# Pool mixer of a two-layer decoder: x kept by features, modulation columns on TensorE, unread products as fillers

## The chip, the core and the metric

The kernel runs on one core of one Trainium2 chip. Its engines are TensorE (PE, with its weight loads shown as PEld), VectorE (DVE), ScalarE (ACT), GpSimd (POOL) and SyncE (SP), which issues most of the loads. The metric is the device time of one execution in microseconds, lower is better. A profile is one further execution, with the hardware profiler on.

## The reference

A decoder of two layers over 512 tokens of 1024 features in fp32. Layer 0 mixes tokens by averages over windows (the pool mixer), layer 1 by a gated unit over chunks (SGU); a squared-ReLU MLP of width 4096 follows each. Shift, scale and gate of every layer come from the condition `c`. What the change touches is layer 0's mixer and the start of its MLP:

```python
mod = silu(c) @ ada_w[i] + ada_b[i]                 # 6 x 1024 numbers
sh1, sc1, g1, sh2, sc2, g2 = split(mod, 6)
h = rmsnorm(x, norm_mix_g[i]) * (1 + sc1) + sh1
# pool mixer: group g of 256 features, window 2, 4, 8, 16 tokens
pooled[g] = mean of the last win tokens of h[g] - h[g]
y = concat(pooled[g] @ pool_w[g]) * pool_scale
x = x + g1 * y
h = rmsnorm(x, norm_mlp_g[i]) * (1 + sc2) + sh2
x = x + g2 * (square(relu(h @ w1[i])) @ w2[i])
```

## The kernel before, in words

Large products are made in fp32 precision out of a rounded high part and a remainder, in three passes (`mm3`: low weights by high data, high by high, high by low). `x` lies in SBUF by tokens, four tiles `X(t)` of 128 tokens by 1024 features in two halves `x_98` and `x_99` (in the code `x_[0]`, `x_[1]`); `xf` is x by features, eight columns `k` of 128 features by 512 tokens.

The stage in question is the mixer, from the start to the first matmul of the MLP of layer 0. It is written in one block whose order is set by hand in two tables: `LOADS` (line 53) names the loads in the order in which SP issues them, `WORK` (line 63) names the pieces of work. A piece is a letter code and digits: `m20` is a modulation column (group 2, number 0), `win2` the window products of group 2, `pd2` their eviction, `pr2` the product with the pool weights, `ad21` the addition into x (group 2, half 1), `sm23` the squares of group 2 in token tile 3, `tn2` the transposes into xf and `td2` their copies, `n00` a column of the MLP's modulation. A suffix V puts a piece on DVE. Each engine runs its own instructions in the order in which the pieces stand. Modulation weights come as 128x1024 tiles into 13 slots (3 `ada`, 5 `wh`, 5 `wl`), and a load is issued when its slot is free.

A *column* (line 694) is one DVE instruction over such a tile: 128 outputs on the partitions, times the row `silu(c)` spread over the partitions (`cb`), summed along the row. Three of the four gate groups are made on PE instead (`gm`, line 720): eight matmuls of 128x256 with `cab` (silu(c) repeated over 128 columns) as weights give the gate by features in a row, the same on all partitions. The fourth (`gt`, `gc`, `bc`) takes two DVE columns and spreads them by a diagonal and a matmul with ones. `we` (743) multiplies gate and pool scale into the pool weights.

The sums of squares of x (`sq`) go to one power on POOL (`rms`), which scales the four bands (`bandr`); a window product is x by tokens times a band. The pooled features, by features, are the weights of `product` (768), which gives tokens by features; `add` (778) adds into x by tokens. Each of x's 256-feature groups is then squared by tokens (`sm`), transposed into xf and copied. The total (`tot`) goes to a second power on POOL, to a diagonal (`diag`) and a spread over all partitions (`rb`). `norm_hi` (854) makes the MLP's operand `ht` and its high part `hb`.

Where PE would wait, `busy` (620) issues matmuls that nobody reads (`BUSY`, line 74: 10 of 128x128, the others 128x256).

Both halves of x are written to DRAM (`spill`, 530) right before the sweep; the last part of layer 0's MLP reads them. The *sweep* runs the first seven of the MLP's 32 column blocks with k outermost: eight steps of 21 matmuls of 512 columns. Each step also needs a raw weight tile, whose high part is copied on ACT (`wh`) and whose low part is made on DVE (`wl`), and two further columns. What follows the sweep is ordered by a planner (`Plan`) from a table of costs, and by the order of the code in layer 1.

In the profile every instruction that goes through the engines' wrapper outside of the planned part has line 107, in the planned part line 135 (102 and 130 in the changed kernel).

Of the kernel before, what the change touches and what calls it, by code (L numbers as in the profile page):

```python
# [7 lines left out]
F32 = mybir.dt.float32  # L8
# [26 lines left out]
V_C, V_ADAB, V_MIX, V_MLP, V_N = 0, 8, 104, 120, 136  # L35
# [10 lines left out]
def c_g(n, k):  # L46
# [18 lines left out]
    pr2 win3 m10 gc1 m11 bc1 ad21 m13 gm0 ad20 sm23 fin1 m33 we1 pd1 win0 m01 sm22 m02 m00 m03 pr1 ad10  # L65
    fin0 pd0 m32 gm3 m30 we0 pr0 m31 fin3 sm10 pd3 ad11 we3 sm21 sm11 hi0 pr3 sm20 ad00 sm13 sm12 sm01
    ad01 sm02 sm03 n00 tn2 sm00 tn0 ad30 s3 ad31 n01 sm30 sm31 sm33 sm32 td2 tot td0 tn3 nf0 n21 n11 tn1
    diag td3 td1 sp0 sp1 lo0
"""


GM = [0, 2, 3]
GT = [1]
BUSY = {"rowc": 10, "gm2": 7, "win2": 3, "gm3": 2, "rb": 2, "sweep": 4}
EARLY = 2

# [277 lines left out]
def decoder_kernel(ctx: ExitStack, tc: tile.TileContext, xtok, vecs, rows, fgrow, ada0, adag, ada1, pool_w, w1s, w1, w1f, w1b, w2, w2e, w_v, w_u, w_o, wsT, lnp, bs, out):  # L354
# [28 lines left out]
    def bank(name, pool=None):  # L383
        pool = pool or ps
        return pool.tile([P, S], F32, name=name, tag="mm" if pool is ps else "xz")
# [184 lines left out]
    with (  # L570
# [5 lines left out]
        for r in range(3):  # L576
            (Y, A)[r > 0].dma_start(row[32 * r : 32 * r + 1], rows[r : r + 1])
# [39 lines left out]
        cab = st.tile([P, KD, P], F32, name="cab")  # L617
        psb = st.tile([P, D], F32, name="psb")

        def busy(name, o, what=None):  # L620

            what = cab.rearrange("p k c -> p (k c)") if what is None else what
            n = min(256, what.shape[-1])
            for _ in range(BUSY.get(name, 0)):
                T.matmul(o[:, 0:n], ones, what[:, 0:n], start=True, stop=True)

        def spread_row(o, r, f):
            for n in range(2):
                pc = bank("pc")
                if (r, n) == (0, 0):  # L630
                    busy("rowc", pc, ones)
                T.matmul(pc, ones[32 * r : 32 * r + 1, :], row[32 * r : 32 * r + 1, S * n : S * n + S], start=True, stop=True)
                A.activation(o[:, S * n : S * n + S], pc, f)

# [3 lines left out]
        def rms():  # L638
            v0 = sm.tile([P, NT], F32, name="rv4", tag="rv4")
            V.tensor_scalar(v0, ss, RMS_EPS, None, ALU.add)  # L640
            rt.append(power(v0, NT))

        def bands():

            for t in range(NT):
                A.activation(bandr[:, t], band[:, 1 if t else 0], AF.Copy, scale=rt[0][:, t : t + 1])
# [7 lines left out]
        def places(name):  # L654

            kind = name.rstrip("0123456789")
            if kind == "n" and int(name[1]) > 1:
                return slots[0:1]
            return [slots[(nslot[0] + j) % len(slots)] for j in range({"ag": 2, "m": 1, "gt": 1, "n": 1}.get(kind, 0))]

        def load(name):
            kind, d = name.rstrip("0123456789"), [int(c) for c in name if c.isdigit()]
            for j, (pool, tag) in enumerate(places(name)):
                r = pool.tile([P, D], F32, name="ada", tag=tag) if pool is w4 else wtile(tag, F32)
                src = {"ag": lambda g: adag[GM.index(g), j], "m": lambda g, q: ada0[4 * g + q], "gt": lambda g, q: ada0[32 + 2 * GT.index(g) + q], "n": lambda k, q: ada0[16 + 2 * k + q]}[kind]
# [35 lines left out]
        pmg = [sm.tile([P, 2], F32, name="pmg", tag=f"pmg{g}", bufs=1) for g in range(4)]  # L701

        def m(g, j):

            column(f"m{g}{j}", pm4[g][:, j : j + 1])

# [8 lines left out]

        pgs, dgs = {}, {}

        def gm(g):  # L720
            po = pgs[g] = bank("pg", xz)[:, 0:256]
            busy(f"gm{g}", po)
            for j in range(2):
                r = take(f"ag{g}", j).rearrange("p (k c) -> p k c", k=4)
                for k in range(4):
                    T.matmul(po, cab[:, 4 * j + k], r[:, k], start=(j + k == 0), stop=False)
            T.matmul(po, ones[32:33, :], row[32:33, 256 * g : 256 * g + 256], start=False, stop=True)

        def gt(g, j):
            column(f"gt{g}{j}", pmg[g][:, j : j + 1])  # L730

        def gc(g):
            pm = pmg[g]
            dg = dgs[g] = st2.tile([P, 2, P], F32, name="dgg", tag="dgg")
            V.tensor_tensor(pm, pm, vec[:, V_ADAB + c_g(0, 2 * g) : V_ADAB + c_g(0, 2 * g) + 2], ALU.add)
            for j in range(2):
                A.activation(dg[:, j], ident, AF.Copy, scale=pm[:, j : j + 1])

        def bc(g):
            pgs[g] = bank("pg", xz)[:, 0:256]  # L740
            T.matmul(pgs[g], ones, dgs.pop(g), start=True, stop=True)

        def we(g):

            gp = st2.tile([P, 256], F32, name="gp", tag="gp")
            V.tensor_tensor(gp, pgs.pop(g), psb[:, 256 * g : 256 * g + 256], ALU.mult)
            c = slice(2 * g, 2 * g + 2)
            V.tensor_tensor(pw[:, c], pw[:, c], gp.unsqueeze(1).to_broadcast([P, 2, 256]), ALU.mult)
# [3 lines left out]
        def windows(g):  # L752

            for k in (2 * g, 2 * g + 1):
                po = pqs[k] = bank("pq")
                if k % 2 == 0:
                    busy(f"win{g}", po)
                for t in range(NT):
                    n = P if t == NT - 1 else W
                    T.matmul(po[:, P * t : P * t + n], X(t)[:, P * k : P * k + P], bandr[:, t, g, 0:n], start=(t == 0), stop=(t == NT - 1), skip_group_check=True)  # L760
# [7 lines left out]
        def product(g):  # L768
            for h in range(2):
                po = pos[g, h] = bank("po", xz).rearrange("p (t c) -> p t c", t=2)  # L770
                for q in range(2):
                    t = 2 * h + q
                    for j in range(2):
                        T.matmul(po[:, q], pds[2 * g + j][:, P * t : P * t + P], pw[:, 2 * g + j], start=(j == 0), stop=(j == 1))

        ssg = st.tile([P, NT, 4], F32, name="ssg")

        def add(g, h):
            c = slice(256 * g, 256 * g + 256)
            V.tensor_tensor(x_[h][:, :, c], x_[h][:, :, c], pos.pop((g, h)), ALU.add)  # L780

        def sums_of(g, t, on=A):
            squares(ssg[:, t, g : g + 1], t, slice(256 * g, 256 * g + 256), on)

        pxs = {}

        def turn(g):
# [3 lines left out]
            for h in range(2):  # L791
                for k in (2 * g, 2 * g + 1):
                    for t in (2 * h, 2 * h + 1):
                        T.transpose(pxs[k][:, P * t : P * t + P], X(t)[:, P * k : P * k + P], ident)
# [4 lines left out]


# [4 lines left out]
        def n_(k, j):  # L805
            if k not in pm2:
                pm2[k] = sm.tile([P, 2], F32, name="pm2", tag="pmv")
            column(f"n{k}{j}", pm2[k][:, j : j + 1])

# [24 lines left out]

        def sum3():
            V.tensor_reduce(s3, ssg[:, :, 0:3], mybir.AxisListType.X, ALU.add)
            V.tensor_scalar(s3, s3, RMS_EPS, None, ALU.add)

        def tot():
            V.tensor_tensor(s3, s3, ssg[:, :, 3], ALU.add)  # L840
            rt.append(power(s3, NT))

        def spread_norms():
            rbs.append(bank("rb", xz))
            busy("rb", rbs[0])
            for t in range(NT):
                r = rt[1][:, t : t + 1]
# [15 lines left out]
        def norm_32(k):  # L863
# [4 lines left out]
            rowc=lambda: spread_row(cb, 0, AF.Silu),  # L868
            rowp=lambda: spread_row(psb, 2, AF.Copy),
            cab=lambda: V.tensor_copy(cab, ca.unsqueeze(2).to_broadcast([P, KD, P])),  # L870
            sq=lambda t, on=A: squares(ss[:, t : t + 1], t, slice(0, D), on),
            sm=sums_of, rms=rms, edge=edges, bandr=bands, m=m, n=n_, nf=n_fin, fin=fin, gm=gm, gt=gt, gc=gc, bc=bc, we=we,
            win=windows, pd=pooled, pr=product, ad=add, tn=turn, td=turned, s=lambda _: sum3(), tot=tot,
# [3 lines left out]
        for op in WORK.split():  # L877
            on_v, op = op.endswith("V"), op.rstrip("V")
# [4 lines left out]

        sweep = [bank("po", xz) for _ in range(SWEEP - 4)] + [bank("po") for _ in range(4)]
        busy("sweep", sweep[0])
        for k in range(KD):
# [14 lines left out]
            norm_32(k)  # L901
            (xh, xl), (wh, wl) = apart(H(k, ALL)), wk[k][1:]
# [761 lines left out]
```

## Time and profile before

| | us |
|---|---|
| three runs: median (lowest to highest) | 824.36 (822.27 to 826.08) |
| the profiled execution | 823.1 |
| its span | 821.4 |
| PE busy in the span | 810.8 (99%) |
| DVE, ACT, POOL busy | 688.1, 484.7, 67.8 |
| first matmul of the sweep | 59.98 |
| end of the sweep in the chain of waits | 97.09 |

The span runs from the first to the last instruction of the program in the profiled execution; the execution's own time has 1.7 us around it. A timeline row merges instructions alike that follow one another ("x16"); an fp32 matmul appears as two entries, a transpose as one. The clock that the profile shows for PE is the granted one; a number in brackets at a row's end is the idle time before it and what ended it.

### The profile page before, as it was taken

The page shows a single profiled execution, that of the slowest core. Times are in us where ns is not written, and L with a number is a line of the kernel's source. Part 1 is how long each engine was busy: PE and PEld are TensorE (multiplying, and loading weights), DVE is VectorE, ACT ScalarE, POOL GpSimd, SP SyncE. Part 2 cuts the span into 40 slices and gives each one's busy share as a digit, 9 for nine tenths or more (in the row PEclk, how much of TensorE's full clock was granted, in tenths as well). Part 3 has the DMA queues.
Part 4 walks back from the last instruction along what each step waited for, and adds up shares of the span by engine and source line. Part 5 has one row for each costly group of instructions (what it writes and reads, how often), then busy time and mean ns, then how long its engine had stood idle before and what let it go on. Part 6 is the DMA issues. An engine that isn't in the chain of part 4 may idle for free.

```text
span 821.4 us, 12594 instructions
## 1 busy us (share of the span) xinstructions
PE 810.8 (99%) x4877; PEld 736.2 (90%) x4877; DVE 688.1 (84%) x924; ACT 484.7 (59%) x704; POOL 67.8 (8%) x93
## 2 busy tenths in 40 slices
PE   9999999999999999999999999999999999999996
PEld 7878889999999999888889888999999999999985
DVE  6889988899998999867798976788789988987865
ACT  4376886675656577257333227676766667677521
POOL 3000001010101010000020001010101000111001
PEclk9999999999999999999999999999999999999999
DMA  9979996889887897526755746947888889777402
GB/s 350 418 286 343 331 273 134 265 219 271 220 277 189 271 254 247 192 103 245 268 171 192 220 161 236 324 98 201 202 255 225 242 220 255 186 175 252 132 26 102
DMA packets 43792, 185.45 MB, mean 226 GB/s; under 512 B 4923, under 2 KB 5075, under 8 KB 36438
## 3 DMA queue, kind: packets, MB, share of 16 engines
q1 hardware_dynamic: 35282, 137.72, 46.1%
q0 software_dynamic: 8016, 44.58, 27.1%
q10 hardware_dynamic: 436, 2.37, 0.8%
q8 instruction: 38, 0.62, 0.3%
q14 instruction: 20, 0.16, 0.1%
HBM read 178.34 MB, written 6.30 MB: 225 GB/s over the span
## 4 chain that ended last, share of the span: by engine, by line
PE 84%; DVE 7%; DMA 3%; ACT 3%; issue 1%; POOL 0%; POOLq 0%; ACTq 0%; DVEq 0%
PE po L107 29%; PE pm L135 18%; PE pm L107 17%; PE po L135 15%; PE pg L107 2%; DMA ada<-in_ada 2%; DVE wl L107 2%; DVE ada L107 2%; DVE v L107 1%; PE pq L107 1%; PE pc L107 1%; DMA raw<-in_w_o 1%; ACT wh L107 1%; PE px L107 1%; ACT hb L107 0%
## 5 line engine op out<-in xcount | busy, mean ns | idle before, releaser
L107 PE MATMUL po<-hb,wh 128*128 128x256 f32 (+1 forms) x816 | 177.4, 314 | 0.0
L107 PEld LDWEIGHTS po<-hb,wh 128*128 128x128 f32 x816 | 134.9, 191 | 8.6 <-DVE hb L107 0.7
L107 PE MATMUL po<-hb,wl 128*128 128x256 f32 (+1 forms) x408 | 128.8, 316 | 0.5 <-DVE wl L107 0.5
L107 DVE TENSOR_TENSOR wl<-raw,wh 128x1024 fp32r<-128x1024 f32 (+2 forms) x85 | 99.0, 1170 | 30.6 <-ACT wh L107 30.3
L107 ACT ACTIVATE wh<-raw 128x1024 fp32r<-128x1024 f32 (+2 forms) x85 | 85.4, 1015 | 53.9 <-PE pm L107 23.4
L107 PEld LDWEIGHTS po<-hb,wl 128*128 128x128 f32 x408 | 77.9, 191 | 5.7 <-PE po L107 0.9
L135 ACT ACTIVATE wh<-raw 128x1024 fp32r<-128x1024 f32 x48 | 50.8, 1058 | 49.3 <-PE pm L135 18.7
L135 PE MATMUL po<-hb,wh 128*128 128x256 f32 (+1 forms) x400 | 78.1, 296 | 0.0
L135 DVE TENSOR_TENSOR wl<-raw,wh 128x1024 fp32r<-128x1024 f32 x48 | 58.3, 1220 | 10.3 <-ACT wh L135 10.0
L135 PEld LDWEIGHTS po<-hb,wh 128*128 128x128 f32 x400 | 63.7, 191 | 2.0
L107 PE MATMUL pm<-wh,oh 128*128 128x512 f32 x188 | 63.8, 357 | 0.0
L135 PE MATMUL pm<-wh,oh 128*128 128x512 f32 x188 | 63.8, 357 | 0.0
L107 PE MATMUL pm<-wh,ol 128*128 128x512 f32 x168 | 63.7, 379 | 0.0
L135 PE MATMUL pm<-wh,ol 128*128 128x512 f32 x168 | 63.7, 379 | 0.0
L135 PE MATMUL pm<-wl,oh 128*128 128x512 f32 x168 | 63.7, 379 | 0.0
L107 PE MATMUL pm<-wl,oh 128*128 128x512 f32 x168 | 63.7, 379 | 0.0
L107 DVE SCALAR_TENSOR_TENSOR ada<-ada,cb 128x1024 f32<-128x1024 f32 x48 | 58.2, 1218 | 4.7 <-DMA ada<-in_ada 4.6
L135 PE MATMUL po<-hb,wl 128*128 128x256 f32 (+1 forms) x201 | 59.3, 296 | 0.0
L107 PE MATMUL po<-as,wh 128*128 128x256 f32 x288 | 49.0, 275 | 0.0
L107 PEld LDWEIGHTS po<-as,wh 128*128 128x128 f32 x288 | 43.7, 192 | 0.0
L135 PE MATMUL po<-as,wh 128*128 128x256 f32 x240 | 40.8, 275 | 0.0
L107 PEld LDWEIGHTS pm<-wh,oh 128*128 128x128 f32 x188 | 35.5, 189 | 5.1
(269 smaller groups left out, 1893.8 us busy)
## 6 DMA issues: line engine op xcount, KB each, us to landing
ada<-in_ada SPq DMA_DIRECT2D x72, 512.0 KB, 4.5
raw<-in_w1b SPq DMA_DIRECT2D x44, 512.0 KB, 5.3
b<-in_w SPq DMA_DIRECT2D x18, 1024.0 KB, 7.1
bt<-in_w POOLq DMA_DIRECT2D x18, 1024.0 KB, 8.3
raw<-in_w1b POOLq DMA_DIRECT2D x22, 512.0 KB, 5.6
raw<-in_w2e SPq DMA_DIRECT2D x16, 512.0 KB, 4.2
bt<-in_w SPq DMA_DIRECT2D x6, 1024.0 KB, 8.7
b<-in_w POOLq DMA_DIRECT2D x6, 1024.0 KB, 9.5
```

Source lines behind the costliest of these rows:

```text
L107: return f(*a, **kw)
L135: self.ops.append((name, attr, lambda: f(*a, **kw), out, ins, kw))
```

## The change

All of it is in the mixer's stage; the sweep's arithmetic and what comes after it are the same.

- x is transposed into xf at the start of the stage (`xt`, `xd`). The product has the pool weights as weights and the pooled features as data (128x512, by features, one k at a time), so gate and pool scale are one number per partition: `add` (k) is a DVE instruction xf = po * gain + xf. `we`, `gm`, `gc`, `bc`, the spread of the pool scale and two of the three row loads are gone; the gate is eight more columns `g0` to `g7`. For the spill, x is transposed back (`bt`) and copied back (`be`).
- A column whose name carries a P in `WORK` (m13, g3, m03, g4, n01, n11) is made on PE: eight matmuls of 32 output rows, with 32 columns of `cab` as weights, at four positions of the array's columns (`tile_position`), two at each, accumulated; an ACT copy (`prt`) and a one-column matmul with `sel` (`whole`) add the four partial sums. Its tile is stored transposed in DRAM.
- Fillers (`z8` and so on) are 128x128 matmuls of ones, written into the next PSUM bank that is opened, 42 in all.
- The sums of squares for the second norm are made by tokens for three groups, and for columns 4 and 5 of group 2 as a square of the full 128x512 column (`sk`) with a matmul by ones (`ss`). First norm and bands go token tile by token tile, with four powers on POOL.
- The loads have a new order: four modulation tiles stand ahead of x. The two spills are issued from ACT at steps 6 and 7 of the sweep.

How this moves instructions on PE at the end of the stage, from the last window products to the sweep. Names: `po` products, `px` transposes, `pg` gates, `pq` windows, `pt` a column on PE, `pm` its sum, `ss` sums of squares, `rb` the spread of the norms; before:

```order
L107 MATMUL po<-pw,pd 128x256 x8
L107 MATMUL pg<-cab,ones 128x256 x2
L107 MATMUL pg<-wl,cab 128x256 x4
L107 MATMUL pg<-wh,cab 128x256 x4
L107 MATMUL pg<-row,ones 128x256
L107 MATMUL po<-pw,pd 128x256 x16
L107 MATMUL px<-ident,x_98 128x128 x4
L107 MATMUL px<-ident,x_99 128x128 x4
L107 MATMUL rb<-cab,ones 128x256 x2
L107 MATMUL rb<-diag,ones 128x128 x4
L107 MATMUL po<-cab,ones 128x256 x4
L107 MATMUL po<-hb,wl 128x512
```

and in the changed kernel:

```order
L102 MATMUL po<-pd,pw 128x512 x4
L102 MATMUL pt<-wl,cab 32x128 x8
L102 MATMUL pm<-sel,prt 128x1
L102 MATMUL px<-ident,xf 128x128 x8
L102 MATMUL ss<-ones,sqk 128x128 x8
L102 MATMUL pt<-wh,cab 32x128 x8
L102 MATMUL px<-ident,xf 128x128 x8
L102 MATMUL pt<-ada,cab 32x128 x8
L102 MATMUL pm<-sel,prt 128x1
L102 MATMUL rb<-ones 128x128 x2
L102 MATMUL rb<-diag,ones 128x128 x4
L102 MATMUL po<-hb,wl 128x512
```

The 32 transposes of x (the pair of px rows stands four times before) have left this place for the start of the stage; transposes back, three columns and the full-column sums stand here now.

On DVE, over the same stretch (`pm`, `mg` sums of columns, `gp` gate times pool scale, `wl`, `wh`, `ada` tiles of columns), before:

```order
L107 TENSOR_TENSOR gp<-pg,psb 128x256
L107 TENSOR_TENSOR pw<-pw,gp 128x512
L107 TENSOR_TENSOR x_98<-x_98,po 128x2x256
L107 TENSOR_TENSOR x_99<-x_99,po 128x2x256
L107 SCALAR_TENSOR_TENSOR wl,pm_484<-wl,cb 128x1024
L107 TENSOR_TENSOR x_98<-x_98,po 128x2x256
L107 TENSOR_REDUCE s_168<-ssg 128x4
L107 TENSOR_SCALAR s_168<-s_168 128x4
L107 TENSOR_TENSOR x_99<-x_99,po 128x2x256
L107 SCALAR_TENSOR_TENSOR ada,pm_484<-ada,cb 128x1024
L107 TENSOR_TENSOR s_168<-s_168,ssg 128x4
```

and in the changed kernel:

```order
L102 SCALAR_TENSOR_TENSOR mg<-mg,vec 128x1
L102 SCALAR_TENSOR_TENSOR xf<-po,mg,xf 128x512
L102 SCALAR_TENSOR_TENSOR mg<-pm,vec 128x1
L102 SCALAR_TENSOR_TENSOR xf<-po,mg,xf 128x512
L102 COPY x_98<-px 128x2x256
L102 SCALAR_TENSOR_TENSOR sq_148,ssg<-x_99 128x256
L102 SCALAR_TENSOR_TENSOR sq_148,ssg<-x_98 128x256
L102 TENSOR_REDUCE s_166<-ssg 128x4
L102 TENSOR_SCALAR s_166<-s_166 128x4
L102 TENSOR_TENSOR s_166<-s_166,ss 128x4
L102 SCALAR_TENSOR_TENSOR wl,pm_593<-wl,cb 128x1024
```

The additions go to xf, each behind its gain; the last one waits for a column that PE made, and only one of the MLP's columns is left on DVE ahead of the norm's spread.

The diff, cut (the two tables to their first lines):

```diff
 LOADS = """
-    x m20 ag2 m22 m21 m23 gt11 pw2 gt10 m12 m10 m13 m11 m33 ag0 m01 pw1 m02 m00 m03 m32 m30 ag3 pw0 m31
-    n11 pw3 raw0 n00 n21 n01 raw1
+    m11 m10 m13 g3 x m12 m33 g2 m31 g7 m30 pw1 m32 m23 m03 pw3 m22 g6 m20 m21 m00 m02 pw2 m01 g5 pw0 g1 g0 g4
+    n01 n00 raw0 n11 raw1
...
-    cab edge sq0 rowc sq2 sq3 sq1V rms m20 m22 rowp m21 m23 gt11 fin2 bandr gm2 win2 we2 gt10 pd2 win1 m12
+    z8 rowc z9 z1 m13P qm13 m11 sq2 g3P m10 sq0V edge z9 z7 xt2 sq1V rms0 rms2 xt1 m12 qg3 gf3 sq3V qm10 rms1
...
-BUSY = {"rowc": 10, "gm2": 7, "win2": 3, "gm3": 2, "rb": 2, "sweep": 4}
+SPIN = 5
 EARLY = 2
+SPILL = (6, 7)
...
         o = pool.tile([P, S], F32, name=name, tag="mm" if pool is ps else "xz")
+        while owed:
+            owed.pop()
+            T.matmul(o[:, 0:P], ones, ones, start=True, stop=True)
...
+        def rms(t):
+            V.tensor_scalar(v0[:, t : t + 1], ss[:, t : t + 1], RMS_EPS, None, ALU.add)
+            G.tensor_tensor(r0[:, t : t + 1], v0[:, t : t + 1], mhalf[:, 0:1], ALU.pow)
...
         def column(name, out):
             r = take(name)
-            V.scalar_tensor_tensor(r, r, 1.0, cb, ALU.mult, ALU.mult, accum_out=out)
+            if name + "P" not in WORK:
+                V.scalar_tensor_tensor(r, r, 1.0, cb, ALU.mult, ALU.mult, accum_out=out)
+                return
+            r = r.rearrange("p (k c) -> p k c", k=KD)
+            pt = bank("pt")[:, 0:P]
+            for k in range(KD):
+                q = 32 * (k % 4)
+                T.matmul(pt[q : q + 32], cab[:, k], r[:, k], start=(k < 4), stop=(k >= 4), tile_position=(0, q), skip_group_check=True)
+            parts_of[name] = st2.tile([P, P], F32, name="prt", tag="prt", bufs=4)
+            A.activation(parts_of[name], pt, AF.Copy)
+        def whole(name, out):
...
+            pm = bank("pm")[:, 0:1]
+            T.matmul(pm, parts_of.pop(name), sel, start=True, stop=True)
...
+        def gain(k):
+            gains[k] = mg[:, KD + k : KD + k + 1]
+            V.scalar_tensor_tensor(gains[k], pmg.pop(k), vec[:, V_ADAB + c_g(0, k) : V_ADAB + c_g(0, k) + 1], vec[:, V_PS + k : V_PS + k + 1], ALU.add, ALU.mult)
...
+        def product(k):
+            pos[k] = bank("po", xz)
+            g = k // 2
+            for j in range(2):
+                T.matmul(pos[k], pw[:, 2 * g + j, P * (k % 2) : P * (k % 2) + P], pds[2 * g + j], start=(j == 0), stop=(j == 1))
+        def add(k):
+            V.scalar_tensor_tensor(xf[:, k], pos.pop(k), gains.pop(k), xf[:, k], ALU.mult, ALU.add)
...
+        def sum_up(k):
...
+            q = sqk.pop(k)
+            for t in range(NT):
+                T.matmul(sums[0][:, tok[t]], q[:, tok[t]], ones, ...)
...
+        def back(g, h):
+            b = pbs[g, h] = bank("px").rearrange("p (t c) -> p t c", t=2)
+            for k in (2 * g, 2 * g + 1):
+                for q in range(2):
+                    T.transpose(b[:, q, P * (k % 2) : P * (k % 2) + P], xf[:, k, tok[2 * h + q]], ident)
...
+        fill(SPIN)
         sweep = [bank("po", xz) for _ in range(SWEEP - 4)] + [bank("po") for _ in range(4)]
-        busy("sweep", sweep[0])
         for k in range(KD):
...
+            if k in SPILL:
+                spill(SPILL.index(k), A)
```

More of the change, by code (lines that the diff above doesn't have):

```diff
@@ L575, in decoder_kernel @@
         row = st.tile([P, D], F32, name="row")
-        for r in range(3):
-            (Y, A)[r > 0].dma_start(row[32 * r : 32 * r + 1], rows[r : r + 1])
+        Y.dma_start(row[0:1], rows[0:1])
         W = P + 16
@@ L714, in fin, with gate, qg @@
             V.scalar_tensor_tensor(b0[:, k], sh, win * (1.0 / win), sh, ALU.mult, ALU.subtract)
[L718 to L748, printed above, removed]
+        def gate(k):
+            pmg[k] = mg[:, k : k + 1]
+            column(f"g{k}", pmg[k])
+        def qg(k):
+            pmg[k] = whole(f"g{k}", pmg[k])
+        def gain(k):
+            gains[k] = mg[:, KD + k : KD + k + 1]
+            V.scalar_tensor_tensor(gains[k], pmg.pop(k), vec[:, V_ADAB + c_g(0, k) : V_ADAB + c_g(0, k) + 1], vec[:, V_PS + k : V_PS + k + 1], ALU.add, ALU.mult)
         pqs, pds, pos = {}, {}, {}
```

154 lines of the change are left out of this document (86 added, 68 removed).

## The prediction, made before the changed kernel ran

> **What bounds the kernel now.** I read the page first, then the chain of waits over the first 110 us, then the windows and timelines of the mixer's stage. The page's first part names the engine:
>
> ```profile
> PE 810.8 (99%) x4877; PEld 736.2 (90%) x4877; DVE 688.1 (84%) x924; ACT 484.7 (59%) x704; POOL 67.8 (8%) x93
> ```
>
> TensorE (PE) is busy for 99% of the span, so time can be won only where PE does work that nothing needs, or before it has real work. That is the mixer's stage: the chain (start, duration, engine, tile; an "x28" counts entries) shows where it ends.
>
> ```profile
> 1.14 8.35 PE pc L107 x28
> 9.48 9.49 PE pg L107 x32
> ...
> 44.69 7.12 PE po L107 x32
> 51.83 0.70 DVE x L107
> ...
> 52.61 0.52 ACT sq L107 x2
> ...
> 53.66 0.98 ACT xf L107 x2
> ...
> 54.69 1.85 PE px L107 x14
> 56.54 1.76 PE rb L107 x12
> 58.30 38.79 PE po L107 x176
> 97.09 12.96 PE po L135 x61
> ```
>
> PE carries the chain almost unbroken to 51.8; then come one addition, squares, copies, transposes and the spread of the norms, and the sweep over the MLP's first seven column blocks begins. Its first matmul is here:
>
> ```profile
> 59.98 0.48 PE L107 MATMUL po<-hb,wl 128*128 128x512 f32 x1
> ```
>
> From 97.09 on the chain is PE alone, and the diff changes nothing after the sweep. So the change is worth what it moves the sweep's start at 59.98 and its end at 97.09. The windows (us; busy PE, PEld, DVE, ACT, POOL; granted clock, DMA share, GB/s) say what the stage is short of:
>
> ```profile
> 45.00:50.00 5.00, 5.00 (x25) 4.41 (x24) 3.15 (x5) 4.81 (x17) 0.00 (x0) 1.00 0.95 385
> 50.00:55.00 5.00, 4.29 (x30) 3.56 (x29) 4.27 (x12) 4.38 (x15) 1.06 (x1) 1.00 0.12 26
> 80.00:90.00 10.00, 10.00 (x48) 8.46 (x47) 10.00 (x17) 6.38 (x15) 0.00 (x0) 1.00 0.97 316
> ```
>
> The loads run to about 50, with the same bytes in both kernels, and PE, DVE and ACT are all loaded; no single engine has much room.
>
> **The change part by part.** The prices, one row for each kind of work (PE first, then DVE, ACT, POOL):
>
> ```profile
> 1.12 4.63 PE L107 MATMUL pc<-ones 128*128 128x128 f32 x20 [1.12 <-DVE edge L107]
> 5.69 3.79 PE L107 MATMUL pc<-row,ones 1*128 1x512 f32 x8
> 24.13 3.62 PE L107 MATMUL po<-pw,pd 128*128 128x256 f32 x16
> 33.48 0.69 PE L107 MATMUL pg<-row,ones 1*128 1x256 f32 x2
> 34.11 2.18 PE L107 MATMUL pq<-bandr,x 128*128 128x144 f32 x16
> 51.63 1.91 PE L107 MATMUL px<-ident,x 128*128 128x128 f32 x16
> 57.24 1.05 PE L107 MATMUL rb<-diag,ones 128*128 128x128 f32 x8
> 33.82 1.22 DVE L107 SCALAR_TENSOR_TENSOR wh<-wh,cb 128x1024 f32<-128x1024 f32 x1
> 34.97 1.22 DVE L107 SCALAR_TENSOR_TENSOR wl<-wl,cb 128x1024 f32<-128x1024 f32 x1
> 51.27 0.17 DVE L107 TENSOR_SCALAR s<-s 128x4 f32<-128x4 f32 x1
> 58.42 0.75 DVE L107 SCALAR_TENSOR_TENSOR ht<-xf,scl,rb 128x512 f32<-128x512 f32 x1 [0.88 <-PE rb L107]
> 5.58 1.06 ACT L107 ACTIVATE sq<-x 128x1024 f32<-128x1024 f32 x1 [2.44 <-DMA x<-in_xtok]
> 14.57 2.78 ACT L107 ACTIVATE bandr<-band,rr 128x576 f32<-128x576 f32 x4 [1.28 <-POOL rr L107]
> 30.65 1.45 ACT L107 ACTIVATE pd<-pq,b,scl 128x512 f32<-128x512 f32 x2 [1.57 <-DVE b L107]
> 50.53 0.42 ACT L107 ACTIVATE sq<-x 128x256 f32<-128x256 f32 x1
> 51.07 0.42 ACT L107 ACTIVATE sq<-x 128x256 f32<-128x256 f32 x1
> 53.57 2.05 ACT L107 ACTIVATE xf<-px 128x512 f32<-128x512 f32 x4
> 55.48 0.50 ACT L107 ACTIVATE mods<-pm,vec 128x1 f32<-128x1 f32 x2
> 56.12 0.70 ACT L107 ACTIVATE diag<-ident,rr 128x128 f32<-128x128 f32 x2
> 65.31 0.95 ACT L107 ACTIVATE wh<-raw 128x896 fp32r<-128x896 f32 x1 [1.92 <-DMA raw<-in_w1s]
> 53.94 1.93 POOL L107 TENSOR_TENSOR rr<-s,mhalf 128x4 f32<-128x4 f32 x1 [39.40 <-DVE s L107]
> 407.22 0.54 POOL L107 TENSOR_TENSOR rr<-rv,mhalf 128x1 f32<-128x1 f32 x1 [26.94 <-DVE rv L107]
> ```
>
> *Unknown price: a modulation column on PE.* Six columns leave DVE (six times 34.97 - 33.82 = 1.15 us) and become eight 32x128 matmuls each, which is 16 entries of 128 columns, with an ACT copy and a one-column matmul behind. A 128-column entry costs 1.91/16 = 0.12 us, so one after another the 16 take about 1.8 us. The nearest row for narrow work is the ones-by-row one: its eight entries of 512 columns fell in the time when 128 columns cost 0.21 us (4.63 for twenty, less the 0.4 in which the last one leaves the array), which would be 8 x 0.85 = 6.8 us; they took 3.79, so two ran at a time. I take two at a time, 0.9 us. Lower bound: four at a time, 0.45. Upper bound: the two entries of 33.48 took 0.69, against 2 x 3.62/16 = 0.45 for full entries of that shape, about 0.1 lost per entry; 16 x (0.11 + 0.1) = 3.3 us.
>
> The Trainium skill, "TensorE: Matmul & The Clock Gate", section "Part 3: Packing small matmuls — row/col tiling", gives 2.38 times the speed for three column tiles side by side; by that an operation here would be nearer 0.6 us (an estimate) and the sum about 1.5 us lower. The trace of before has no column tiles to set against it.
>
> *PE's opening.* PE starts at 1.14 as before. Eight fillers (16 entries x 0.21 = 3.4) and two row matmuls instead of four (3.79/2 = 1.9) end at 6.4, ten more fillers at 10.7; a column at that slow rate (1.8), one between the rates (1.2) and 16 fillers (32 x 0.11 = 3.5, once the entries are as short as in the px row) end at about 17, and ACT gets the first turned x at 17.2. x is loaded after four 512 KB tiles instead of first: its first tile was there at 5.58, and seven tiles more at 385 GB/s (1.36 us each) make the last one land at 15.1. That costs nothing behind those fillers, which leave it 2 us; without them PE would wait for it.
>
> *Transposes, bands, first windows.* From about 17.2 ACT has eight xf copies (2.05/4 = 0.51) and four bandr (2.78/4 = 0.70), 6.9 us: to 24.1. Of this the copies are new here (they stood at 53.57 and 57 before). The powers tile by tile (0.54 and more each on POOL, instead of 1.93 for four) end long before, beside the fillers. Seven windows that wait for the last band, at 2.18/8 = 0.27 less the overlap, 1.7, and four products of two 512-column entries (twice 3.62/16 an entry, less the overlap, so 0.86 each), 3.4, come next: to 29.2. A filler and a column, 0.2 + 0.9, to 30.3; two products, 1.7, to 32.0.
>
> *What goes.* 24 full matmuls for the gates with their rows, the diagonal and its spread, and four products with the pool weights on DVE go; they were PE's filling rather than its limit, because DVE still owes its columns.
>
> *DVE's stretch.* Two additions into xf at the price of ht (0.75 in the record, of which 0.66 until DVE takes the next), six columns at 1.15, seven small operations around the two `fin` at 0.17 or less, together 1.0, and hand-overs, 0.3: 1.3 + 6.9 + 1.3 = 9.5, to 41.5.
>
> *ACT's stretch.* Two pd (0.72), six squares (51.07 - 50.53 = 0.54), two copies back and one full-column square (0.51 each): 1.4 + 3.2 + 1.5 = 6.1, to 47.6. ACT takes its work in order: the copy of gate column 4 is queued behind these squares, and PE's matmul, DVE's gain and the last addition wait for it. Copy 0.35 (half of the diag row), one-column matmul 0.3 and gain 0.25 (as half of the mods row), addition 0.75: 1.65, to 49.3.
>
> *Tail.* Last square 0.6; eight sums with ones 1.05 (as the rb row); column 0.9, eight transposes 0.95, column 0.9; copy, copy, diagonal 0.35 + 0.25 + 0.35; spread 0.9; one-column matmul 0.3; copy, x copied back, hb 0.25 + 0.5 + 0.7. That is 8.0, to 57.3, and 0.2 for hand-overs: 57.5. POOL's power of 1.93 runs beside the columns and transposes. Loads do not decide: the same bytes end at about 50, and n01 and n11 are used after 51. The start moves from 59.98 to about 57.5, **-2.5 us**.
>
> *The sweep.* It took 37.1. At 80 to 90 it ran 48 entries in 10 us, so its 168 need 35.0 or somewhat more; the excess comes with the wait of 1.92 for the second weight tile, when two 1 MB spills stand ahead of it. The spills now go at steps 6 and 7, and the raw tile can land first. Bounds 0 and -1.9; I take **-0.8**. Sum: -3.3 us.
>
> *The moved spills.* Two issues on ACT at about 0.4 us stand in steps in which ACT is busy 6.38 of 10; what is queued behind is the next step's hb. The 2 MB meet a DMA share of 0.97: at 316 GB/s 6 us of transfer. Hidden by loads that are issued early it costs 0; without that cover PE would wait for part of it, half as an estimate, +3.
>
> **The rivals.** *Four columns at a time.* The column tiles have a quarter of the array each, and the ones-by-row entries already doubled up. At 0.45 us the five columns in the chain (two in the opening, one before 30.4, two in the tail) save 5 x 0.45 = 2.2 us more, less 0.3 that the first row of x hides: sweep from about 55.6, total -5.2, 818.5 us. Against it: no row shows more than two.
>
> *One after another.* At 1.8 the five add 4.5 us: start 62.0, less 0.8 in the sweep a total of +1.2: 824.9 us. For it: both entries of one matmul use the same quarter of the array one after the other; against it, the 3.79.
>
> *Slower: narrow matmuls lose their weight load.* If a weight load for another strip waits until the matmul in flight is out, as the 0.69 for two entries hints, an operation takes 3.3 us; five add 12 us, sweep from about 69.5, less 0.8 a total of +8.7: 832.4 us. Five operations pass the bound of +4.1 from about 0.9 + 7.4/5 = 2.4 us each on. Against it: 3.79 us for eight, on narrow tiles too.
>
> The Trainium skill, same page and section, says that a weight load overlaps matmuls in flight only when the row group differs; column tiles share their rows. "TensorEngine Tiling (Array Packing)", section "Key Properties", adds that a change of tiling mode drains TensorE. By these rules this rival would be the outcome; only the row of 33.48 agrees, at 0.1 us per entry, and the row of 3.79 does not.
>
> *The gain is eaten later.* The stage ends earlier but the loads behind the sweep land when they did, or the spills delay them: 0 net, 823.7 us. For it: the DMA share of 0.97 at 80 to 90; against it: the chain behind 97.09 shows PE alone and no transfer.
>
> **How the numbers follow.** The profiled execution took 823.1 us around a span of 821.4; the three runs have their median at 824.36, so I start from between, 823.7, and -3.3 gives 820.4. A measurement of this kernel can tell about 0.5%, 4.1 us, from no change. Chances: forecast 0.47 (over its spread of 2 us to either side about a third lies beyond -4.1), four at a time 0.20, one after another 0.12, weight loads 0.12, eaten 0.09. Faster: 0.20 + 0.17 = 0.37. Slower: 0.12 and 0.02 for the upper edge of the serial case, 0.14. Same: 0.49. The range leaves out the fastest edge of the four-fold case (start below 55 and a full 1.9 in the sweep, under 815) and the weight-load case above 829, which starts at 827.8 for 2.4 us: 815 to 829.
>
> **What would show it.** In the trace after: `pt` of eight 32x128 matmuls in 0.9 us (0.45, 1.8, 3.3 for the rivals); sweep's first `po<-hb,wl` at 57.5; ACT's second `wh<-raw` in the sweep without the wait of 1.92; the sweep's end near 93.8; PE unbroken afterwards. I am wrong if `pt` takes over 2 us, if ACT ends its squares after 49, or if the start moves and the finish does not.

## The result, and the profile after

The changed kernel takes 822.72 us (median of 20 runs, 820.76 to 825.90), the kernel before 824.09 (20 runs, 822.26 to 826.99): ratio 0.9989, 95% interval 0.9976 to 1.0002. The forecast of -3.3 us was not met: -1.4 us between the medians, not clear of zero. The forecast time of 820.4 lies below the measured median, which lies inside the stated range of 815 to 829.

The profiled execution of the changed kernel is one of its slower ones (825.6 us, span 823.9). No profile was taken of a faster execution of it. Its windows, with the columns of those shown of before:

```profile
50.00:55.00 5.00, 4.80 (x50) 4.18 (x50) 4.54 (x12) 3.70 (x12) 0.87 (x1) 1.00 0.05 20
90.00:95.00 5.00, 4.65 (x21) 3.50 (x21) 5.00 (x7) 4.04 (x6) 0.00 (x0) 1.00 0.92 347
95.00:100.00 5.00, 2.97 (x15) 2.32 (x14) 3.83 (x5) 3.46 (x6) 0.00 (x0) 1.00 1.01 397
```

The last of these windows in the kernel before:

```profile
95.00:100.00 5.00, 5.00 (x26) 4.37 (x25) 5.00 (x6) 5.00 (x10) 0.00 (x0) 1.00 0.99 416
```

The stage's end still has idle DMA queues (0.05), and PE now has a hole at 95 to 100, where before it was busy throughout. PE's timeline shows the stage's terms one by one:

```profile
4.83 3.78 PE L102 MATMUL pc<-row,ones 1*128 1x512 f32 x4
8.54 4.43 PE L102 MATMUL pt<-ones 128*128 128x128 f32 x20
12.90 0.65 PE L102 MATMUL pt<-ada,cab 128*32 128x128 f32 x16
18.50 1.91 PE L102 MATMUL px<-ident,x 128*128 128x128 f32 x16
24.51 4.05 PE L102 MATMUL pq<-bandr,x 128*128 128x144 f32 x28 [0.45 <-ACT bandr L102]
32.16 0.64 PE L102 MATMUL pt<-wl,cab 128*32 128x128 f32 x16
32.73 1.98 PE L102 MATMUL po<-pd,pw 128*128 128x512 f32 x4
51.57 2.09 PE L102 MATMUL ss<-ones,sqk 128*128 128x128 f32 x16
59.52 0.48 PE L102 MATMUL po<-hb,wl 128*128 128x512 f32 x1 [0.33 <-ACT hb L102]
```

A column on PE takes 0.57 us (32.16 to 32.73), and the two row matmuls take as long as the four did before (3.78 against 3.79). The sweep starts at 59.52, only 0.46 earlier. Its end is worse. The chain of waits and ACT's timeline there:

```profile
81.82 6.51 DMA ada<-in_ada
...
89.62 6.85 DMA raw<-in_w
96.54 1.06 ACT wh L130
...
99.08 11.07 PE po L130 x51
```

```profile
96.54 1.06 ACT L130 ACTIVATE wh<-raw 128x1024 fp32r<-128x1024 f32 x1 [2.03 <-DMA raw<-in_w]
97.51 1.04 ACT L130 ACTIVATE as<-xf 128x1024 fp32r<-128x1024 f32 x1
98.45 3.02 ACT L130 ACTIVATE g<-po 128x512 f32<-128x512 f32 x6
```

ACT waits 2.03 us for a raw tile of the part behind the sweep; the evictions of the sweep's results (`g<-po`) are queued behind that copy, and PE waits for the banks that they free. The first matmul behind the sweep's 168 stands at 99.08, against 96.93 before. The tile was issued at almost the same moment in both (89.62 and 89.48) and landed after 6.85 us instead of 4.67: the two spills were issued beside it, at 89.63 and 91.29. In all the profiles below, what follows the sweep takes 723.7 to 725.9 us, so a profile's span is set by where its sweep ends, to within about 2 us.

### The profile page after: what moved, and what is told of

It reads as the page before. It is cut to its first block, busy times and chain, and to the rows that moved or that the text cites. A ratio compares the mean times of both kernels' runs of the same rounds, so it can differ in the third digit from the quotient of the medians.

```text
span 823.9 us, 12793 instructions
## 1 busy us (share of the span) xinstructions
PE 808.9 (98%) x4969; PEld 729.9 (89%) x4969; DVE 689.3 (84%) x936; ACT 484.7 (59%) x703; POOL 70.4 (9%) x96
## 4 chain that ended last, share of the span: by engine, by line
PE 86%; DVE 7%; DMA 3%; ACT 2%; issue 1%; POOL 0%; POOLq 0%; DVEq 0%; ACTq 0%
PE po L102 32%; PE pm L130 18%; PE pm L102 17%; PE po L130 15%; DVE ada L102 2%; DVE wl L102 2%; DMA ada<-in_ada 1%; PE px L102 1%; PE pt L102 1%; PE pc L102 1%; DMA raw<-in_w 1%; DVE wh L102 1%; ACT wh L102 1%; PE pq L102 0%; DVE ht L102 0%
## 5 line engine op out<-in xcount | busy, mean ns | idle before, releaser
L102 PEld LDWEIGHTS po<-hb,wl 128*128 128x128 f32 x408 | 77.9, 191 | 5.6 <-ACT hb L102 1.3
L102 DVE SCALAR_TENSOR_TENSOR ada<-ada,cb 128x1024 f32<-128x1024 f32 x50 | 60.6, 1220 | 12.7 <-DMA ada<-in_ada 7.3
L130 PEld LDWEIGHTS po<-hb,wl 128*128 128x128 f32 x201 | 38.4, 191 | 3.4 <-ACT g L130 2.4
```

Source lines behind the costliest of these rows:

```text
L102: return f(*a, **kw)
L130: self.ops.append((name, attr, lambda: f(*a, **kw), out, ins, kw))
```

## The experiments

Sweep start and end are read from the entries on PE (the first entry, and the first behind the 168 of the sweep), as is the moment at which PE's entries become half as long ("rate up"); this moment is good to one entry, about 0.2 us. Pauses are the times from one PE entry's start to the next, added up where they are far above the regular 0.22, within the sweep and at its end. All in us, with the span of the profiled execution; the ratio is to the kernel before as measured beside the run. A row's medians come from 6 to 20 executions (one in e4 and e10), its other times from a single one, which is not always near the median.

| kernel | median | ratio (95%) | rate up | sweep start | pauses | sweep end | span |
|---|---|---|---|---|---|---|---|
| before | 824.09 | | 13.9 | 59.98 | 0 | 96.93 | 821.4 |
| changed | 822.72 | 0.9989 (0.9976-1.0002) | 12.6 | 59.52 | 3.1 | 99.08 | 823.9 |
| e1 | 822.84 | 0.9989 (0.9977-1.0002) | 5.5 | 57.75 | 0.7 | 94.73 | 818.7 |
| e2 | 823.64 | 1.0004 (0.9994-1.0014) | 5.7 | 60.65 | 0.7 | 97.66 | 823.6 |
| e3 | 822.28 | 0.9986 (0.9973-1.0000) | 12-13 | 57.28 | 2.3 | 96.36 | 820.7 |
| e4 | 833.67, one run | | 13.1 | 67.61 | 2.1 | 106.19 | 832.0 |
| e5 | 822.36 | 0.9982 (0.9974-0.9991) | 6.8 | 56.87 | 3.1 | 96.39 | 821.3 |
| e6 | 824.40 | 1.0008 (0.9992-1.0023) | 4.7 | 56.49 | 3.0 | 96.40 | 821.0 |
| e7 | 823.85 | 1.0002 (0.9991-1.0012) | 4.1 | 59.61 | 1.2 | 97.79 | 821.9 |
| e8 | 823.41 | 0.9995 (0.9979-1.0010) | 14 | 60.04 | 2.2 | 99.01 | 823.3 |
| e9 | 822.28 | 0.9986 (0.9975-0.9998) | 5.6 | 56.74 | 2.5 | 95.93 | 819.8 |
| e10 | 826.34, one run | | 4.7 | 61.65 | 2.8 | 100.61 | 824.6 |
| e11 | 819.34 | 0.9948 (0.9930-0.9967) | 4.7 | 56.76 | 0 | 93.31 | 817.0 |
| e12 | 822.49 | 0.9981 (0.9969-0.9993) | 6.4 | 56.68 | 1.6 | 94.56 | 818.3 |

The diffs below are shortened to the lines that matter.

**e1 and e2: is it the spills' place?** e1 is the changed kernel, e2 the kernel before.

```diff
 e1:  ... diag nf0 qn11 be20
+     sp0 sp1
-            if k in SPILL:
-                spill(SPILL.index(k), A)
 e2:  diag td3 td1 sp0 sp1 lo0   ->   diag td3 td1 lo0
+            if k in (6, 7):
+                spill(k - 6, A)
```

> The changed kernel with its two spills issued right ahead of the sweep, as before, instead of at steps 6 and 7. Theory 1 (the spills in the sweep take the DMA queues from the loads behind it): the two pauses of PE at the sweep's end in the changed kernel's profile (0.73 us before 92.06, 2.41 us before 99.08) go, the wait for the second raw tile near 65 comes back and costs PE 0.3 us at most, and the time falls by about 2.5 us to 819.5 to 821. Rival (the pauses are the loads' own scatter, which the spills have no part in): pauses like these appear again, and the time stays at 822.7 within 0.7.

> The kernel before with its two spills moved to steps 6 and 7 of the sweep, and nothing else. Theory 1: PE, unbroken there before, pauses for 2 to 3 us between step 7 and the end of the sweep, waiting for raw and ada tiles; the time rises to about 826. Rival: the sweep ends at 97 as before or 0.5 earlier (no wait of 1.92 near 65), the time stays at 824.1 or falls to 823.5.

The theory of the spills alone fell: by the medians e1 is no faster than the changed kernel, and e2 no slower than the kernel before. e1's profile, of one of its fastest executions (820.43), has the shorter pauses and the early end (94.73), but the sweep also *started* 1.8 us earlier, which the edit doesn't explain: PE's rate had risen at 5.5 instead of 12.6. The same rows in e1, to be set against those at 4.83 and 8.54 above:

```profile
4.83 2.27 PE L102 MATMUL pc<-row,ones 1*128 1x512 f32 x4
7.04 2.50 PE L102 MATMUL pt<-ones 128*128 128x128 f32 x20
```

Twenty entries take 2.50 us there and 4.43 in the changed kernel, with the windows' clock at 1.00 in both. That is a second cause, and it differs between executions whose opening is the same. In e2's profile, too, the rate rose early (5.7). There PE then waited 1.88 us for a gate tile, the granted clock read 0.50 from 29.5 to 32.8, and the sweep started at 60.65, later than before.

**e3: the opening.** Spills as in e1, row halves on two partitions, 16 fillers left out.

```diff
-        Y.dma_start(row[0:1], rows[0:1])
+        Y.dma_start(row[0:1, 0:S], rows[0:1, 0:S])
+        A.dma_start(row[64:65, S:D], rows[0:1, S:D])
-                T.matmul(pc, ones[0:1, :], row[0:1, S * n : S * n + S], start=True, stop=True)
+                T.matmul(pc, ones[64 * n : 64 * n + 1, :], row[64 * n : 64 * n + 1, S * n : S * n + S], start=True, stop=True)
-    ... sq0V edge z9 z7 xt2
+    ... sq0V edge xt2
```

> The changed kernel with three edits: spills ahead of the sweep; the two halves of the row of c on partitions 0 and 64, loaded by two queues, so that the two row matmuls can run side by side (3.78 us for the two in the changed kernel); and the 16 fillers ahead of the first transposes left out. Theory 2 (the stage is one chain of DVE work from about 20.6 to 51, and DVE stood idle 3.7 us before it, for a sum on PE behind those 16 fillers, after 5.3 us of waiting for cb, so each microsecond taken off PE's opening comes off the sweep's start): cb 1.8 us earlier, the idle 3.7 us gone but for 0.5, the sweep starts at 55 to 56.5 instead of 59.5, and with the spills the time is 816 to 818. Rival (the loads or the clock set the stage's end): the sweep starts at 58.5 to 60 all the same, because DVE then waits for tiles or PE falls to half clock, and only the spills' 2.5 us remain.

The start came 2.2 us earlier with a late rise (57.28, of which 1.2 us are a wait, 0.33 in the changed kernel: the spills' issues on ACT stand ahead of the first `hb`). So the chain through DVE is real. But the pauses in the sweep grew to 2.3 us and the time hardly moved: 822.28 instead of the expected 816 to 818. The rows on two strips:

```profile
4.83 2.08 PE L102 MATMUL pc<-row,ones 1*128 1x512 f32 x4
```

**e4: one strip.**

```diff
-                T.matmul(pt[q : q + 32], cab[:, k], r[:, k], start=(k < 4), stop=(k >= 4), tile_position=(0, q), skip_group_check=True)
+                T.matmul(pt[0:32], cab[:, k], r[:, k], start=(k == 0), stop=(k == KD - 1), tile_position=(0, 0))
```

> The changed kernel with the eight 32x128 matmuls of a PE column all at one position of the array (one strip of columns, one accumulation) instead of four positions in turn. By the prediction's terms: if the positions run side by side, the operation's 16 entries now take 16 x 0.11 = 1.75 us instead of 0.65, more (up to 3.3) if a load of weights for the same strip isn't hidden; the two operations in the tail move the sweep's start by 2 x 1.1 = 2.2 us, the other ones by less than 1 us. If the strips have no part in it: 0.65 us as now and no move.

```profile
13.11 1.93 PE L102 MATMUL pt<-ada,cab 128*32 128x128 f32 x16
```

1.93 against 0.65: four positions do run side by side. The start moved by 8.1 us, not 2.2: that fits six columns in the chain (6 x 1.3 = 7.8), where the expectation had two and the prediction five.

**e5, e7, e8: the rate.** e5 has 17 fillers ahead of the rows and the rows on two strips; e7 is the kernel before with 17 fillers; e8 the changed kernel again.

```diff
 e5: -    z8 rowc z9 z1 m13P        +    z9 z8 rowc z1 m13P      (and e3's rows)
 e7: -BUSY = {"rowc": 10, ...       +BUSY = {"rowc": 17, ...
```

> The changed kernel with its opening rearranged: 17 fillers ahead of the row matmuls instead of 8, one between them and the first column instead of 10, and the row's two halves on partitions 0 and 64. In the traces so far PE's entries halve in length at 5.3 to 5.6 us in two executions and at 12.5 to 13.9 in the others; the one-row matmuls stand between. Theory 3 (the rate rises after one unbroken stretch of full matmuls that fills a window of its own phase; with 8 fillers the rows break it in most executions, and the changed kernel gains only where it doesn't): with 7.2 us of fillers the rate rises by 8.4 in every execution; sweep starts at 56.5 to 57.5 (59.5 in the changed kernel's profile), the runs lose their upper group (824 to 826), median 821.0 to 821.6. Rival (the two groups of run times come from the loads in and behind the sweep): rise by 8.4 all the same, but the times spread as before over 820.8 to 825.9, median 822.7 within 0.6.

> The kernel before with 17 instead of 10 fillers ahead of its row matmuls and nothing else. In the one trace of it with the early rise PE then waited for gate tiles (0.61 at 11.48, 1.88 at 28.82) and the sweep started no earlier (60.65 against 59.98). Theory 3: the rate rises by 8.4, PE waits for loads instead, sweep start 60 to 61, time 823.7 within 0.7: the early rise is worth something to the changed kernel alone. Rival: the kernel before gains as much as the changed one, 2 to 3 us, sweep start 57 to 58.

> The changed kernel once more, for its scatter beside the others on the same chip. Theory 3: its profile shows either a rise at about 5.3 and a sweep start near 56.8, or a rise at about 12.7 and a start near 59.5, and the times lie in two groups, 820.5 to 822.5 and 824 to 826. Rival: the start doesn't follow the rise.

The first rows of e5's timeline:

```profile
1.12 6.85 PE L102 MATMUL pc<-ones 128*128 128x128 f32 x34 [1.12 <-DVE edge L102]
7.90 1.13 PE L102 MATMUL pc<-row,ones 1*128 1x512 f32 x4
8.96 0.49 PE L102 MATMUL pt<-ones 128*128 128x128 f32 x2
```

In all seven profiles with 17 full matmuls first (e5 to e7, e9 to e12) the rate rises at 4.1 to about 7; in the seven others twice early and five times at 12 to 14. The upper group of times is gone in e5 (821.08 to 823.17, against 821.07 to 827.66 in e8), and the start is 2.6 to 3.2 us earlier than in the two profiles of the changed kernel. e5 also has the rows on two strips, so not all of this is the rate; but e1, with an early rise and its rows on one strip, started at 57.75 with 0.8 us more of a wait for the spills' issues, and so would have started like e5 without it (56.9, an estimate). e7 gains nothing: it starts 0.4 earlier and its PE waits for gate tiles instead. So by these profiles the early rise is worth something only where PE's next tiles are there. But e5's median, 822.36, missed its 821.0 to 821.6: again 3.1 us of pauses at the end.

The Trainium skill ("TensorE: Matmul & The Clock Gate", section "Part 1: The HAM clock gate (the "warmup" mystery)") puts the array at half clock until one window of about 3.4 us has been busy, and lets these windows run free of the kernel's start. The runs agree where full matmuls stand alone: 17 fillers span two such windows (6.8 us) and the rise comes by 7; with 8 or 10 (3.4 and 4.3 us) it came early in two profiles of seven. But the kernel before kept PE busy without a gap from 1.12 on, and its rate rose only at 13.9, with the one-row matmuls at 5.69 to 9.48. That these don't count as busy is my inference; it wasn't tried alone.

**e6 and e9: where the spills collide least.** e6 is e5 without the 16 fillers, spills after the sweep's first step. e9 is e5 with half 0 spilled when it is turned back, half 1 behind the first `hb`.

```diff
 e6: -    z8 rowc z9 z1 m13P qm13 m11 sq2 g3P m10 sq0V edge z9 z7 xt2
     +    z9 z8 rowc z1 m13P qm13 m11 sq2 g3P m10 sq0V edge xt2
     +            if k == 0: spill(0, A); spill(1, A)
 e9: -    ... be21 bt20 qn00 n11P qn01 z2 diag nf0 qn11 be20
     +    ... be20 bt21 qn00 n11P qn01 z2 diag nf0 sp0 qn11 be21
     +            norm_hi(k); if k == 0: spill(1, A)
```

> As the kernel with the clock first, and besides the 16 fillers ahead of the first transposes left out and both spills issued from ACT at the end of the sweep's first step (ahead of the sweep they held up the first hb by 1.1 us, at steps 6 and 7 they may meet the next loads). Theory 3 with DVE's chain: first transposes at 14.7 when x lands, sweep starts at 55.5 to 56.5, 1 us ahead of the kernel with the clock first, time 819.5 to 821. Rival (x's landing and the bands hold the stage): sweep starts as in the kernel with the clock first, within 0.3.

> The kernel with the clock first (e5), and its spills where the DMA queues have nothing: half 0 issued as soon as it is turned back (the transposes back of the last group change places), half 1 right behind the sweep's first hb, which it doesn't hold up. Theory 4 (from the sweep's start the queues are full at a share of 0.9 to 1.0, so 2 MB of spill inside the sweep turn an earlier start into pauses at its end: 56.87 in e5 became 96.39, 57.75 with the spills ahead became 94.73): start at 56.9 to 57.3, pauses of 0 to 0.7 us, sweep's end at 94 to 95, the times in one group around 820.5, ratio 0.995 to 0.997. Rival (the pauses belong to the loads of an earlier start, wherever the spills are): pauses of 2 to 3 us in the sweep again, end at 96 to 97, times around 822.4 as in e5.

Starts of 56.5 and 56.7 became ends of 96.4 and 95.9; moving the spills only moved the pauses (to 66 to 72 and to 91). Theory 4 fell. Leaving out the 16 fillers brought 0.4 us at the start of e6's sweep, and the clock fell: PE waited three times for x (0.8 to 0.9 us each), and from about 12 to 18 its windows read 0.50:

```profile
12.00:14.00 2.00, 0.64 (x2) 0.18 (x1) 1.97 (x7) 1.05 (x2) 0.00 (x0) 0.50 1.04 424
14.00:16.00 2.00, 1.77 (x9) 1.77 (x10) 2.00 (x6) 1.26 (x5) 0.49 (x1) 0.50 1.02 416
```

e6's median of 824.40 lies above its profiled execution (822.71); whether falls like this one cost its other executions more stays open. e9's windows:

```profile
50.00:55.00 5.00, 5.00 (x64) 4.13 (x63) 3.49 (x12) 3.96 (x13) 1.94 (x1) 1.00 0.20 52
65.00:70.00 5.00, 3.98 (x19) 3.15 (x19) 3.31 (x6) 1.28 (x3) 0.00 (x0) 1.00 1.03 419
```

The queues are nearly idle at 50 to 55 and full at 65 to 70, where PE and DVE stand.

**e10: what the PE columns are worth.** e5 with the P taken off all six names.

> The kernel with the clock first (e5) with its six PE columns back on DVE (m13, g3, m03, g4, n01, n11), and nothing else changed. By the DVE chain of the stage five or six columns at 1.15 us lie in it: sweep start 56.87 + 5.5 to 7 = 62.4 to 64, time about +5 us against e5. If DVE has slack in the stage: start within 1 us of e5's.

The start moved by 4.8 us: less than 5.5, and less than six columns of 1.15 (6.9). But this is not the price of the columns alone. With less to do, PE waits more, and its granted clock fell three times, the last time across the sweep's start:

```profile
15.00:18.00 3.00, 3.00 (x16) 3.00 (x16) 2.97 (x10) 1.19 (x2) 0.20 (x1) 0.50 1.03 421
22.00:25.00 3.00, 3.00 (x14) 3.00 (x15) 2.96 (x8) 3.00 (x6) 1.06 (x1) 0.50 1.01 400
59.50:62.70 3.20, 3.20 (x15) 3.02 (x15) 2.72 (x5) 1.94 (x5) 0.00 (x0) 0.50 0.57 187
```

The last ten filler entries ahead of the sweep took 2.34 us there and 1.36 in the changed kernel. How the 4.8 us divide between DVE and the clock is not shown, and 0.6 of the pauses listed for e10 are an entry at half rate. The one run, 826.34, lies above all 15 runs of the kernel before beside it (822.03 to 825.99).

**e11 and e12: fewer bytes in the sweep.** On e9 and on e5:

```diff
-    n01 n00 raw0 n11 raw1
+    n01 n00 raw0 n11 raw1 n10 raw2 n20 n21
-            if kind == "n" and int(name[1]) > 1:
+            if kind == "n" and int(name[1]) > 2:
-                nslot[0] += kind != "n" or d[0] <= 1
+                nslot[0] += kind != "n" or d[0] <= 2
-            r = st2.tile([P, D], F32, name="raw", tag="raw")
+            r = st2.tile([P, D], F32, name="raw", tag="raw", bufs=3)
```

> The kernel of e9 (clock first, spills from 54 on) with three column tiles (n10, n20, n21) and the raw tile of step 2 loaded at the end of the mixer's stage, where the DMA share was 0.12 to 0.20 at 50 to 55, into slots that are free there (n20 and n21 in weight slots instead of the three column slots, a third buffer for raw tiles): 1.5 to 2 MB less in the sweep. Theory 5 (since e9's early start became 2.5 us of pauses, at 66.8, 71.7 and 90.8, wherever the spills stood, the sweep's end is set by the bytes that must come between 54 and 96): pauses below 0.8 us in sum, sweep from 56.7 to 93.8, against 95.9 in e9; times 820.0 to 820.7, ratio about 0.996. Rival (the pauses are single late tiles, not bytes): the end stays at 95.5 to 96.5 and the times at 822.3.

> The same preload in the kernel of e5, with the spills at steps 6 and 7 as in the changed kernel. Theory 5: the first six steps run without a pause and the next loads are issued earlier, but the 2 MB of the spills still stand ahead of the planned part's first raw tiles: pauses of 0.5 to 2 us at 89 to 95 (3.1 in e5), end at 94.5 to 95.5, times about 821.3. Rival: as e5, end at 96.4, 822.4.

e11 is faster than the kernel before by 0.52% (0.33% to 0.70%), and its interval lies below the changed kernel's; 819.34 is also below the 820.0 that was expected at best. Its windows and its chain:

```profile
50.00:55.00 5.00, 5.00 (x64) 4.13 (x63) 3.50 (x12) 3.97 (x13) 1.94 (x1) 1.00 0.63 239
55.00:60.00 5.00, 4.67 (x27) 3.85 (x27) 4.80 (x7) 4.04 (x9) 0.00 (x0) 1.00 1.00 365
65.00:70.00 5.00, 5.00 (x24) 4.36 (x24) 5.00 (x10) 3.33 (x7) 0.00 (x0) 1.00 0.97 365
```

```profile
56.76 36.72 PE po L102 x168
93.48 6.70 PE po L130 x32
```

The share at 50 to 55 is 0.63 instead of 0.20, and the sweep is one piece without a pause. e12's profile keeps the first seven steps unbroken and has a pause of 1.6 us at the end, behind the spills at steps 6 and 7. It is of the fastest of its 12 executions (820.03); the median, 822.49, is that of the rival. Read together, four kernels with one opening separate the two edits: neither (e5) 0.9982, the spills' place alone (e9) 0.9986, the preload alone (e12) 0.9981, both (e11) 0.9948. So only both together help: fewer bytes between the stage's end and 96, and no spill beside the next part's raw tile. That tile lands 6.5 to 7.1 us after its issue in the seven profiles with spills at steps 6 and 7, and 4.3 to 4.7 us after it in e1, e7 and the kernel before.

## Why the prediction was wrong

**The opening.** The term "two row matmuls instead of four (3.79/2 = 1.9)" failed. The four before stood on two strips and ran in pairs; the two that are left share one strip and run one after the other, 3.78 (on two strips in e3, 2.08). I read the pairing as one of the entries of a matmul. The rise came at 12.6 and added nothing here, and the two cheaper columns gave back about 1 us; the first turned x was copied at 19.14 instead of 17.2. With errors both ways from there on, the stage kept about this lateness of 1.9 us: it was 2.7 at the start and the end of DVE's stretch, 2.1 at the end of ACT's and 2.0 at the sweep's start (59.52 against 57.5).

**The column on PE.** Taken at 0.9, measured 0.57: the rival with four at a time was the right mechanism, and the rivals with 1.8 and 3.3 are out. The two rules of the Trainium skill ("TensorE: Matmul & The Clock Gate", section "Part 3: Packing small matmuls — row/col tiling", and "TensorEngine Tiling (Array Packing)", section "Key Properties") by which the slower rival would have been the outcome hardly show here. With the same rows, the 16 entries with their weights took 0.65 us at four column positions and 1.93 at one, so the loads of weights for other columns did not wait. Between narrow and full matmuls entries start 0.20 us apart, against 0.11 among full ones: at most 0.1 us for a change of mode.

**The middle.** The windows behind the last band were 14 (28 entries, 4.05 us), not seven (1.7), partly made up by ACT's copies and bands, which took less than 6.9. DVE's stretch was right: it began late, but from 34.75 to 44.19, where ACT takes the next pd, it is 9.4 us against 9.5 (the first and the last of its rows):

```profile
34.75 0.75 DVE L102 SCALAR_TENSOR_TENSOR xf<-po,mg,xf 128x512 f32<-128x512 f32 x1 [0.75 <-PE po L102]
44.00 0.15 DVE L102 SCALAR_TENSOR_TENSOR b<-mods 128x2 f32<-128x2 f32 x1
```

So was ACT's, 44.19 to the copy of gate column 4 at 49.75, 5.6 against 6.1:

```profile
44.19 1.45 ACT L102 ACTIVATE pd<-pq,b,scl 128x512 f32<-128x512 f32 x2 [2.33 <-DVE b L102]
49.75 0.28 ACT L102 ACTIVATE prt<-pt 128x128 f32<-128x128 f32 x1
```

**The tail.** The term "eight sums with ones 1.05 (as the rb row)" was half the price: eight fp32 matmuls are 16 entries, 2.0 us; the rb row held four.

**The sweep.** "I take -0.8" is the step that failed most. The wait of 1.92 near 65 did go, but the sweep took 39.6 us instead of 37.0, because the third raw tile behind it, with the spills beside it, landed 2.3 us later (96.46 against 94.15 before). I priced the moved spills at nothing, as "Hidden by loads that are issued early"; the cover was not there, and the sweep grew by 2.6, near the +3 that I named for that case. e1 and e9 add that another place for the spills would not have saved the time by itself, and e12 that fewer bytes in the sweep would not either. "Loads do not decide" held for the changed kernel's stage and not for its sweep, and the rival in which the gain is eaten later, to which I gave 0.09, is nearest to what happened. The kernel before had almost no room there either: its own wait for that tile was 0.44 us, hidden from PE.

```profile
94.23 1.06 ACT L135 ACTIVATE wh<-raw 128x1024 fp32r<-128x1024 f32 x1 [0.44 <-DMA raw<-in_w]
```

Where the time went, then: in executions with a late rise, the stage gains about 0 to 0.5 us and the sweep's end loses 2; with an early one it gains about 3 and the loads take back most of it. The late case is shown by the changed kernel's two profiles, the early one by e5, and e11 shows what it is worth without the loss. The changed kernel itself was never profiled with an early rise; how often its executions have one is only inferred from its times.

## What to carry to other kernels

Before an earlier start is counted as a gain, look at what its next consumer waits for: a DMA share near 1.0 behind the changed place warns that the end there may be set by bytes, and the idle share just ahead of it (0.05 to 0.20 here) is where those bytes belong. Count entries, not matmuls, when a price is carried from one row to another, and see which rows ran side by side before halving one. Where a kernel's opening depends on PE's rate, an unbroken stretch of full matmuls of about 7 us made the rise early in 7 of 7 profiles; shorter fillers with one-row matmuls between them did in 2 of 7. And fillers go on being worth something later: in e2, e6 and e10 PE waited and its clock fell to half again.

## What the runs showed of the hardware that I had not expected

- PE's entries take twice as long until between 4 and 14 us from the start (0.213 against 0.111 us for 128 fp32 columns); with one and the same opening the rise came at 5.5 in e1 and at 12.6 to 14 in the changed kernel, e4 and e8. The granted clock of the windows reads 1.00 throughout this stretch, so only the length of equal entries shows it. Later falls do stand in that column.
- The clock falls again without PE being idle for long: in e2 it had stood still for 1.88 us, in e6 for 0.8 to 0.9 us three times, before windows that read 0.50.
- Four 128x32 column tiles with their own weights start 6 to 7 ns apart, and two fp32 passes for eight of them take 0.65 us, against 1.93 at one position.
- One-row fp32 matmuls on two strips run in pairs, 2.08 for four entries of 512 columns at half rate, and 3.78 on one strip.
